# A written-out schedule with other prices for VectorE and GpSimd, and a regrouped softmax in sparse attention

## The chip, the cores and the metric

The kernel runs on one core of a Trainium2 chip. The metric is the device time of one execution in microseconds. One core has a matrix engine (TensorE, PE in the profile, with its weight loads as PEld), VectorE (DVE), ScalarE (ACT), GpSimd (POOL) and a queue for transfers (SyncE, SP). Each runs its own list of instructions in order, and an instruction waits for semaphores of the others.

## The reference

Two blocks of a transformer on 1024 positions of width 1024, in 32-bit floats. The first has two layers, each with two kinds of dense attention, a convolution and a gate; the second has a gated linear attention, an attention over keys that an indexer selects, and a feed-forward part. Cut to what the change touches, the sparse attention is this:

```python
def dsa_attention(q, ckv, iq, ik, iw):
    top_k = min(TOPK_MAX, L // 4)
    ...
    def one_block(args):
        s = jax.nn.relu(jnp.einsum('bqhd,bsd->bqhs', iq_b, ik).astype(jnp.float32))
        score = jnp.einsum('bqh,bqhs->bqs', iw_b.astype(jnp.float32), s)
        score = jnp.where(causal[None], score, -jnp.inf)
        _, idx = lax.top_k(score, top_k)
        kv_sel = jax.vmap(lambda c, i: c[i])(ckv, idx)
        logits = jnp.einsum('bqhc,bqkc->bqhk', q_b, kv_sel).astype(jnp.float32) * (dc ** -0.5)
        probs = jax.nn.softmax(logits, axis=-1).astype(kv_sel.dtype)
        return jnp.einsum('bqhk,bqkc->bqhc', probs, kv_sel)
```

It has 16 heads of a latent width of 128. The kernel computes it with masks in place of gathered keys.

## The kernel before

Activations lie transposed, features on the 128 partitions and positions along the columns, in pages (`pg`) of 128x512. Every operand of a matmul is split into a rounded part and a remainder (`split`, L720): a copy that rounds (a CAST in the profile, on VectorE or ScalarE) and a subtraction (`lo`), and a product is three matmuls. The subtraction runs on VectorE where the source is in PSUM, and on VectorE or GpSimd where it is in SBUF.

The program isn't written in the order in which it runs. Each helper records an operation with a price in microseconds for every engine that could run it (`alts`: t TensorE, a ScalarE, v VectorE, p GpSimd, d a transfer), what it reads and writes, and how to emit it. `schedule` (L406) then plays the whole program with these prices: each engine takes the earliest ready operation by its place in the text, within a window, if its buffers are free. An operation that two engines could run is left to the cheaper one if waiting for that would end earlier. The order that comes out is what is emitted; the chip then runs each engine's list in that order.

The prices are made in `c_act` (ScalarE, L266), `copy` (L302), `c_v` (VectorE, L314), `c_p` (GpSimd, L317), `scale` (L357), `red` (L370) and `vec` (L375). `LAT` (L485) is the time from an operation's end until another engine sees it. `o.dual` (L221) marks an operation that VectorE may run, that reads no PSUM and that has a source of over 64 columns; while GpSimd is busy, such an operation is priced longer:

```python
                    if e == "v" and o.dual and busy["p"] > now:
                        c += 0.42 * min(busy["p"] - now, c / 0.58)
```

The stages in order of time, roughly: first norm, modulation and convolution of block 1 (to 400 us), the two dense attentions of its first layer (`attend`, L1075; 350 to 900), the second layer (900 to 1800, its attentions 1200 to 1700), the indexer's scores and the search for the largest (1850 to 2300), run beside the gated linear attention, sparse attention (2300 to 2960), its projection and a norm (to 3140), the feed-forward part (to 3890) and a last gated addition with a norm (to the end). In the attentions a unit is a head and a chunk of 512 positions; a unit has a lead, a loop and an end, and the lead of the next unit is merged into the loop of this one (`pipeline`, L258).

In sparse attention (from L1757) a unit is a head and a half (c) of the 1024 positions. For each of four blocks of 128 queries (t) and one or two blocks of keys (b), the lead computes scores in PSUM, adds the mask and takes the maximum in one VectorE instruction (L1796, CUSTOM_DVE_ANT_0 with a read of the accumulator), makes -max/sqrt(128) (L352), the exponentials with their sums on ScalarE (L289), a reciprocal of the sum (L1807), and scales the probabilities by it (L365 on VectorE, L363 on ScalarE). Where there are two blocks of keys, two more operations of one column join the maxima and the sums (L330). The loop transposes the probabilities on TensorE (L393), splits them and multiplies by the values; the end adds two halves of the sum into `ob`, which is written out.

## Time and profile before

| | |
|---|---|
| median of 3 runs | 3984.7 us (3984.07 to 3984.71) |
| the profiled execution, its own time | 3984.33 us |
| its span, first to last instruction | 3982.5 us |
| busy: TensorE, VectorE, ScalarE, GpSimd | 97%, 79%, 49%, 38% of the span |
| mean granted TensorE clock | 0.99 of full speed |

Busy time is the union of an engine's instructions. A matmul's span in the profile holds its pipeline, so matmuls that follow each other overlap, and a TensorE that is busy all the time need not be at its peak. In the rows, L330 is an addition, subtraction or product of two tensors on VectorE and L332 the same on GpSimd; L340 multiplies by a column or tensor and adds or multiplies a second; L298 is a copy on VectorE; L373 a reduction; L389 a matmul and L393 a transpose. A tile's name is its kind: `pg` a page in SBUF, `ps` a PSUM bank, `sm` a small tile, `c` a constant.

### The profile page before, as it was taken

What the parts mean: (1) busy time and instruction counts of PE and PEld (TensorE: products, weight loads), DVE (VectorE), ACT (ScalarE), POOL (GpSimd) and SP (SyncE); (2) the same over time, 40 slices, a digit from 0 to 9 for tenths busy, and PEclk for the clock granted to TensorE, in tenths of its full rate; (3) what the DMA queues carried; (4) which work ended last, traced back from release to release, by engine and by line L of the source; (5) the groups of instructions that cost most, each with busy time, mean ns of one, the idle gap of its engine ahead of it and who ended that gap; (6) DMA issues with size and microseconds to landing.
All of it is one profiled execution on the core that took longest, in us unless ns stands there. A gap on an engine that the chain in (4) does not pass through costs nothing. (4 is left out here: it accounts for less than half of the span.)

```text
span 3982.5 us, 53245 instructions
## 1 busy us (share of the span) xinstructions
PE 3860.4 (97%) x18344; PEld 3100.5 (78%) x18344; DVE 3130.6 (79%) x5241; ACT 1964.9 (49%) x3841; POOL 1520.0 (38%) x1348
## 2 busy tenths in 40 slices
PE   6999999999999999999999999999999999999997
PEld 4778777768878777678988888877778788888876
DVE  8998899996796888857988985788776854446598
ACT  5345577763245566635355731566653432222255
POOL 7654465561252444522354531111143511111177
PEclk8999999999999999999999999999999999999998
DMA  7232222133232110232111332000054411111121
GB/s 247 82 119 79 63 68 65 47 115 135 69 121 72 31 30 20 87 116 73 57 55 60 126 111 77 29 29 34 25 191 127 146 42 49 51 51 43 49 86 57
DMA packets 184975, 311.82 MB, mean 78 GB/s; under 512 B 22912, under 2 KB 46208, under 8 KB 184704
## 3 DMA queue, kind: packets, MB, share of 16 engines
q1 hardware_dynamic: 184704, 308.42, 23.6%
q8 instruction: 144, 2.36, 0.2%
q14 instruction: 127, 1.04, 0.1%
HBM read 237.81 MB, written 62.39 MB: 75 GB/s over the span
## 5 line engine op out<-in xcount | busy, mean ns | idle before, releaser
L389 PE MATMUL ps<-pg,pg 128*128 128x512 f32 (+5 forms) x17008 | 3789.5, 384 | 43.6 <-ACT pg L289 19.8
L389 PEld LDWEIGHTS ps<-pg,pg 128*128 128x128 f32 (+3 forms) x17008 | 2955.4, 188 | 733.5 <-issue 72.9
L332 POOL TENSOR_TENSOR pg<-pg,pg 128x512 fp32r<-128x512 f32 (+4 forms) x1030 | 1437.2, 1411 | 2015.2 <-ACT pg L289 1037.8
L289 ACT ACTIVATE pg<-pg 128x512 fp32r<-128x512 f32 (+7 forms) x1385 | 785.7, 596 | 779.4 <-DVE pg L340 252.1
L289 ACT ACTIVATE pg<-ps 128x512 f32<-128x512 f32 (+10 forms) x1352 | 681.8, 551 | 870.3 <-PE ps L389 708.2
L330 DVE TENSOR_TENSOR pg<-pg,pg 128x512 fp32r<-128x512 f32 (+7 forms) x839 | 769.5, 930 | 150.9 <-ACT pg L289 99.2
L330 DVE TENSOR_TENSOR pg<-ps,pg 128x512 fp32r<-128x512 f32 (+9 forms) x650 | 367.5, 584 | 223.3 <-PE ps L389 133.9
L340 DVE SCALAR_TENSOR_TENSOR pg<-ux,c,pg 128x512 f32<-128x512 f32 x416 | 361.4, 895 | 22.5 <-ACT pg L289 13.9
L373 DVE TENSOR_REDUCE sm<-ps 128x1 f32<-128x512 f32 (+1 forms) x492 | 326.5, 681 | 26.8 <-PE ps L389 23.5
L298 DVE CAST pg<-pg 128x512 fp32r<-128x512 f32 (+4 forms) x342 | 210.9, 623 | 56.2 <-ACT pg L289 24.9
L340 DVE SCALAR_TENSOR_TENSOR pg<-pg,c,pg 128x512 f32<-128x512 f32 (+3 forms) x242 | 223.9, 962 | 5.6 <-ACT pg L289 4.9
L289 ACT ACTIVATE pg<-ps,c 128x512 f32<-128x512 f32 (+1 forms) x182 | 128.0, 708 | 202.9 <-PE ps L389 162.9
L393 PE MATMUL ps<-c,pg 128*128 128x128 f32 (+1 forms) x796 | 163.8, 272 | 11.4 <-DVE pg L298 6.0
L1541 DVE MAX8 sm<-ux 128x8 f32<-128x384 f32 (+5 forms) x192 | 166.9, 884 | 1.3
L1542 DVE MATCH_REPLACE8 ux<-sm,ux 128x384 f32<-128x384 f32 (+5 forms) x192 | 167.4, 875 | 0.0
L298 DVE COPY ux<-ps 128x512 f32<-128x512 f32 x79 | 54.5, 691 | 140.3 <-ACT pg L289 122.6
L389 PE MATMUL ps<-pg,c 128*128 128x512 f32 (+3 forms) x196 | 81.7, 482 | 54.8 <-DVE pg L330 21.7
L393 PEld LDWEIGHTS ps<-c,pg 128*128 128x128 f32 (+1 forms) x796 | 103.9, 141 | 37.9 <-DVE pg L298 6.0
L289 ACT ACTIVATE pg<-pg,sm 128x512 f32<-128x512 f32 (+2 forms) x192 | 116.3, 607 | 18.8 <-DVE sm L352 18.4
L678 ACT ACT_TABLE_LOAD x92 | 118.0, 1283 | 1.6
L383 POOL MEMSET pg<- 128x128 f32 (+2 forms) x193 | 49.9, 274 | 159.7 <-PE ps L389 99.0
L1796 DVE CUSTOM_DVE_ANT_0 pg<-ps,pg 128x512 f32<-128x512 f32 (+3 forms) x176 | 98.8, 573 | 11.6 <-PE ps L389 10.7
(73 smaller groups left out, 1024.7 us busy)
## 6 DMA issues: line engine op xcount, KB each, us to landing
d<-pg SPq DMA_DIRECT2D x202, 256.0 KB, 2.0
pg<-d SPq DMA_DIRECT2D x178, 256.0 KB, 3.5
pg<-in_w2a SPq DMA_DIRECT2D x108, 256.0 KB, 3.0
pg<-in_wmod SPq DMA_DIRECT2D x96, 256.0 KB, 3.3
pg<-in_wup SPq DMA_DIRECT2D x88, 256.0 KB, 2.7
pg<-in_win SPq DMA_DIRECT2D x80, 256.0 KB, 3.4
pg<-in_wout SPq DMA_DIRECT2D x64, 256.0 KB, 3.3
pg<-in_wdn SPq DMA_DIRECT2D x48, 256.0 KB, 2.7
```

The costliest lines, as they stand in the source:

```text
L289: nc.scalar.activation(real(out), real(in_), fn, scale=real(scale), **k)
L298: self.nc.vector.tensor_copy(real(out), real(in_))
L330: self.nc.vector.tensor_tensor(out=real(out), in0=real(in0), in1=real(in1), op=o)
L332: self.nc.gpsimd.tensor_tensor(out=real(out), in0=real(in0), in1=real(in1), op=o)
L340: self.nc.vector.scalar_tensor_tensor(out=real(out), in0=real(in0), scalar=real(scalar), in1=real(in1), op0=o0, op1=o1)
L373: lambda e: self.nc.vector.tensor_reduce(out=real(out), in_=real(in_), axis=AX.X, op=o))
L389: lambda e: self.nc.tensor.matmul(real(out), lhsT=real(lhsT), rhs=real(rhs), start=start, stop=stop))
L393: lambda e: self.nc.tensor.transpose(real(out), real(in_), real(ident)))
L678: nc.scalar.preload_act_table_set(pre)
L1541: P.vec(P.c_v(n), [w], [m8], lambda e, m8=m8, w=w: nc.vector.max(real(m8), real(w)))
L1542: P.vec(P.c_v(n), [w, m8], [w], lambda e, m8=m8, w=w: nc.vector.match_replace(real(w), real(m8), real(w), MARK))
L1796: lambda e, p=p, s=s, n=n, m=mk[t, b], a=sm[:, b:b + 1]: nc.vector.tensor_tensor_reduce(out=real(p), in0=real(s[:, 0:n]), in1=real(m), sca ...
```

## The change

Three things are edited. First, the prices: VectorE's, ScalarE's and GpSimd's fixed parts get smaller (an addition of 512 columns on VectorE goes from 0.687 to 0.599 us, on GpSimd from 1.326 to 1.218), and a new table `TAIL` adds a time after which the result counts as done, which doesn't hold the engine. Second, the rule for VectorE and GpSimd: `hold` is the time until which either holds the other off, and an operation of the one that is priced while the other holds is made longer by what is left. Reductions and what `vec` records (the largest-8 search, masked maxima, scans) don't take part. And GpSimd takes an operation that VectorE could run only if VectorE has enough ready work of the kind that takes no part. Third, sparse attention: one small tile holds the numbers of the four blocks; the maximum over two blocks of keys is carried by the second masked maximum, whose start value is the first's result; -max, the sum of two and the reciprocal are one operation for four blocks. The probabilities are no longer scaled. Instead the reciprocals are spread over 64 rows by four transposes into a PSUM bank, copied into a page `rr`, and multiplied into `ob` once for two heads.

```diff
     def c_act(self, n, src, extra=0):
-        return (n * 0.836 + (170 if isinstance(src, View) and src.psum else 202) + extra) / 1000
+        return (n * 0.836 + (49 if isinstance(src, View) and src.psum else 93) + extra) / 1000
...
     def c_v(self, n, ex=0):
-        return (n * 1.04 + 155 + ex) / 1000
+        return (n * 1.04 + 67 + ex) / 1000
 
     def c_p(self, n):
-        return (n * 2.2 + 200) / 1000
+        return (n * 2.2 + 92) / 1000
...
     def vec(self, cost, reads, writes, emit):
 
-        return self.op({"v": cost}, reads, writes, emit)
+        o = self.op({"v": cost}, reads, writes, emit)
+        o.dual = False
+        return o
...
+        TAIL = {"t": 0.0, "a": 0.115, "v": 0.083, "p": 0.08, "d": 0.0}
+        hold = {"v": 0.0, "p": 0.0}
...
                                 if wait + o.alts[m] < o.alts[e]:
                                     ok = False
+                                elif e == "p" and m == "v":
+
+                                    apart = sum(x.alts["v"] for _, x in ready["v"][:6] if not issued[x.idx] and not x.dual)
+                                    if hold["v"] <= now:
+                                        apart += max(0.0, busy["v"] - now)
+                                    if len(ready["v"]) > 1 and apart + o.alts["v"] < o.alts["p"] + max(0.0, hold["v"] - now):
+                                        ok = False
...
-                    if e == "v" and o.dual and busy["p"] > now:
-                        c += 0.42 * min(busy["p"] - now, c / 0.58)
+                    if e == "p" or e == "v" and o.dual:
+                        other = "p" if e == "v" else "v"
+                        c += max(0.0, hold[other] - now)
+                        hold[e] = now + c
...
-                        fin = now + c
+                        fin = now + c + TAIL[e]
...
+                sm = P.buf("sm", (128, 4, 4), F32)
+                nb = 1 + c
                 for t in range(4 * c, 4 * c + 4):
                     qs = slice((t % 4) * 128, (t % 4) * 128 + 128)
-                    sm = P.buf("sm", (128, 4, 4), F32).rearrange("p a b -> p (a b)")
-                    nb = 1 if t < 4 else 2
+                    top = sm[:, 0, t % 4:t % 4 + 1]
...
-                    if nb == 2:
-                        P.tt(sm[:, 0:1], sm[:, 0:1], sm[:, 1:2], "max")
-                    P.ts(sm[:, 2:3], sm[:, 0:1], -(128.0 ** -0.5), None, "mult")
+                P.ts(sm[:, 0, :], sm[:, 0, :], -(128.0 ** -0.5), None, "mult")
+                for t in range(4 * c, 4 * c + 4):
                     for b in range(nb):
-                        P.act(pn[t, b], pn[t, b], "Exp", bias=sm[:, 2:3], scale=128.0 ** -0.5, accum=sm[:, 4 + b:5 + b])
-                    if nb == 2:
-                        P.tt(sm[:, 4:5], sm[:, 4:5], sm[:, 5:6], "add")
-                    P.vec(0.08, [sm], [sm], lambda e, sm=sm: nc.vector.reciprocal(real(sm[:, 6:7]), real(sm[:, 4:5])))
-                    for b in range(nb):
-                        P.scale(pn[t, b], pn[t, b], sm[:, 6:7])
+                        P.act(pn[t, b], pn[t, b], "Exp", bias=sm[:, 0, t % 4:t % 4 + 1].k("e"), scale=128.0 ** -0.5,
+                              accum=sm[:, 1 + b, t % 4:t % 4 + 1].k((t, b)))
+                if nb == 2:
+                    P.tt(sm[:, 1, :], sm[:, 1, :], sm[:, 2, :], "add")
+                P.vec(0.2, [sm], [sm], lambda e, sm=sm: nc.vector.reciprocal(real(sm[:, 3, :]), real(sm[:, 1, :])))
...
+                rp = P.ps()
+                for t in range(4):
+                    P.tr(rp[0:64, t * 128:(t + 1) * 128], sm[:, 3, t:t + 1].to_broadcast([128, 64]), ident)
                 if i == 0:
-                    ob[c] = P.pg()
+                    ob[c], rr[c] = P.pg(), P.pg()
+                P.copy(rr[c][G, :].k(i), rp[0:64, :])
...
                 if i == 1:
+                    P.tt(ob[c], ob[c], rr[c], "mult", "vp")
                     obd[hp, c] = P.dram((128, 512))
```

What the planner makes of it shows in the order of the instructions on an engine. The end of GpSimd's list is the last norm, in which a page's mean is taken off and squares are summed; these are its last ten operations before:

```order
L332 TENSOR_TENSOR pg_38516<-pg_38516,pg_38649 128x256
L332 TENSOR_TENSOR pg_38675<-pg_38394,pg_38675 128x256
L332 TENSOR_TENSOR pg_38701<-pg_38409,pg_38701 128x256
L332 TENSOR_TENSOR pg_38516<-pg_38516,pg_38704 128x256
L332 TENSOR_TENSOR pg_38510<-pg_38510,pg_38698 128x256
L332 TENSOR_TENSOR pg_38510<-pg_38510,pg_38701 128x256
L332 TENSOR_TENSOR pg_38457<-pg_38457,pg_38724 128x256
L332 TENSOR_TENSOR pg_38549<-pg_38549,pg_38724 128x256
L332 TENSOR_TENSOR pg_38675<-pg_38675,pg_38724 128x256
L332 TENSOR_TENSOR pg_38701<-pg_38701,pg_38724 128x256
```

And these are its last ten in the change:

```order
L332 TENSOR_TENSOR pg_38142<-pg_38045,pg_38142 128x256
L332 TENSOR_TENSOR pg_37728<-pg_37728,pg_38174 128x256
L332 TENSOR_TENSOR pg_38217<-pg_38052,pg_38217 128x256
L332 TENSOR_TENSOR pg_38270<-pg_38063,pg_38270 128x256
L332 TENSOR_TENSOR pg_38166<-pg_38166,pg_38314 128x256
L332 TENSOR_TENSOR pg_38320<-pg_38079,pg_38320 128x256
L332 TENSOR_TENSOR pg_38162<-pg_38162,pg_38318 128x256
L332 TENSOR_TENSOR pg_38162<-pg_38162,pg_38320 128x256
L332 TENSOR_TENSOR pg_38122<-pg_38122,pg_38352 128x256
L332 TENSOR_TENSOR pg_38320<-pg_38320,pg_38352 128x256
```

Of the last eight subtractions of a mean (a tile with itself and one common tile: 38724 before, 38352 after) GpSimd had four and has two; the rest of its ten operations lie further back in the change than before.

In the attention of block 1's first layer, VectorE's list holds reductions of scores in PSUM (L373), splits of pages, and the modulation of the next layer (L340). Between two such reductions of the same unit it reads before (`sm` is the unit's tile of maxima):

```order
L298 CAST pg_7414<-pg_7401 128x512
L373 TENSOR_REDUCE sm_7390<-ps_7406 128x1
L298 CAST pg_7433<-pg_7408 128x512
L373 TENSOR_REDUCE sm_7390<-ps_7419 128x1
L330 TENSOR_TENSOR pg_7454<-pg_7079,pg_7138 64x512
L373 TENSOR_REDUCE sm_7390<-ps_7426 128x1
L330 TENSOR_TENSOR pg_7441<-pg_7441,pg_6388 64x512
L373 TENSOR_REDUCE sm_7390<-ps_7436 128x2
```

And in the change, for the same unit:

```order
L298 CAST pg_7478<-pg_7443 128x512
L373 TENSOR_REDUCE sm_7417<-ps_7437 128x1
L330 TENSOR_TENSOR pg_7497<-pg_7415,pg_7470 128x512
L373 TENSOR_REDUCE sm_7417<-ps_7445 128x2
L330 TENSOR_TENSOR pg_7514<-pg_7443,pg_7478 128x512
L373 TENSOR_REDUCE sm_7417<-ps_7455 128x1
L330 TENSOR_TENSOR pg_7528<-pg_7461,pg_7492 128x512
L373 TENSOR_REDUCE sm_7417<-ps_7474 128x1
```

The subtractions of the split (L330 of 128x512), which stood on GpSimd's list, now stand between the reductions on VectorE's.

In sparse attention, VectorE's list at the end of one unit's lead reads before (`sm` holds one block's numbers):

```order
L330 TENSOR_TENSOR sm_26012<-sm_26012 128x1
L330 TENSOR_TENSOR pg_26172<-ps_26102,pg_26164 64x512
L1807 RECIPROCAL sm_26012<-sm_26012 128x1
L330 TENSOR_TENSOR sm_26047<-sm_26047 128x1
L365 TENSOR_SCALAR pg_26011<-pg_26011,sm_26012 128x512
L1807 RECIPROCAL sm_26047<-sm_26047 128x1
L298 CAST pg_26191<-ps_26070 128x512
L365 TENSOR_SCALAR pg_26057<-pg_26057,sm_26047 128x384
```

And in the change (`sm` holds four blocks' numbers):

```order
L298 COPY pg_26431<-ps_26394 64x512
L330 TENSOR_TENSOR pg_26085<-ps_26394,pg_26431 64x512
L330 TENSOR_TENSOR pg_26085<-pg_26085,pg_26047 128x512
L298 CAST pg_26459<-ps_26415 128x512
L330 TENSOR_TENSOR sm_26284<-sm_26284 128x4
L330 TENSOR_TENSOR pg_26468<-ps_26411,pg_26457 128x512
L330 TENSOR_TENSOR pg_26474<-ps_26415,pg_26459 128x512
L1825 RECIPROCAL sm_26284<-sm_26284 128x4
L330 TENSOR_TENSOR pg_26484<-ps_26433,pg_26464 128x512
```

One addition and one reciprocal of four columns stand there instead of those of one column, the scalings (L365) are gone, and the third row is the product of `ob` with the reciprocals.

## Rows read from the trace of the kernel before

**Rows 1.** Stretches: length; busy us (count): PE, PEld, DVE, ACT, POOL; clock; DMA.

```profile
0.00:400.00 400.00, 357.79 (x1737) 284.40 (x1738) 366.18 (x484) 187.92 (x343) 233.21 (x173) 0.96 0.39 131
700.00:800.00 100.00, 99.53 (x442) 72.68 (x442) 95.89 (x160) 78.29 (x151) 52.64 (x47) 1.00 0.15 44
1300.00:1700.00 400.00, 395.24 (x1627) 283.43 (x1627) 339.38 (x538) 257.22 (x476) 185.22 (x180) 1.00 0.15 45
2500.00:2900.00 400.00, 390.83 (x2140) 318.85 (x2139) 320.50 (x1095) 255.83 (x664) 48.50 (x87) 1.00 0.09 30
3300.00:3400.00 100.00, 100.00 (x443) 82.81 (x442) 51.66 (x66) 30.60 (x48) 19.05 (x20) 1.00 0.16 51
3800.00:3900.00 100.00, 92.00 (x380) 72.36 (x379) 94.60 (x89) 50.57 (x80) 83.40 (x52) 0.95 0.17 53
3900.00:3982.50 82.50, 53.41 (x394) 49.81 (x392) 71.82 (x98) 44.90 (x86) 55.09 (x52) 0.81 0.18 61
```

**Rows 2.** The same for ten us with matmuls of 256 columns.

```profile
3940.00:3950.00 10.00, 10.00 (x86) 10.00 (x85) 8.74 (x12) 2.98 (x9) 9.36 (x12) 1.00 0.24 71
```

**Rows 3.** Groups of TensorE, 1300:1700: count | busy, mean ns | idle before.

```profile
L389 PE MATMUL ps<-pg,pg 128*128 128x512 f32 x878 | 308.5, 459 | 2.4 <-DVE pg L298 1.1 <-ACT pg L289 0.9 <-POOL pg L332 0.3
...
L389 PE MATMUL ps<-pg,pg 97*128 97x512 f32 x108 | 42.7, 421 | 0.1
```

**Rows 4.** Timeline of the tail: start, us, engine, operation, count.

```profile
3802.58 0.43 DVE L298 CAST pg<-pg 128x512 fp32r<-128x512 f32 x1 [0.81 <-POOL pg L332]
...
3888.52 0.74 DVE L340 SCALAR_TENSOR_TENSOR pg<-pg,c,pg 128x512 f32<-128x512 f32 x1
3888.67 8.53 POOL L332 TENSOR_TENSOR pg<-pg,pg 128x512 fp32r<-128x512 f32 x5 [0.36 <-DVE pg L298]
3889.18 6.87 DVE L340 SCALAR_TENSOR_TENSOR pg<-pg,pg 128x512 f32<-128x512 f32 x4
...
3897.68 0.68 DVE L340 SCALAR_TENSOR_TENSOR pg<-pg,pg 128x512 f32<-128x512 f32 x1
```

**Rows 5.** Timeline in the first layer's attention.

```profile
732.76 1.32 POOL L332 TENSOR_TENSOR pg<-pg,pg 128x512 fp32r<-128x512 f32 x1 [0.97 <-ACT pg L289]
...
732.96 1.89 DVE L373 TENSOR_REDUCE sm<-ps 128x2 f32<-128x512 f32 x3
```

**Rows 6.** Groups of VectorE and GpSimd, 500 to 900 us.

```profile
L340 DVE SCALAR_TENSOR_TENSOR pg<-pg,c,pg 128x512 f32<-128x512 f32 x72 | 69.9, 982 | 0.2
L298 DVE CAST pg<-pg 128x512 fp32r<-128x512 f32 x62 | 42.5, 690 | 5.3 <-ACT pg L289 4.6
...
L332 POOL TENSOR_TENSOR pg<-pg,pg 128x512 fp32r<-128x512 f32 x128 | 183.3, 1439 | 140.0 <-DVE pg L298 52.8 <-ACT pg L289 52.6 <-PE ps L389 14.9
```

**Rows 7.** Groups of small operations and scalings, 2500 to 2900 us, sparse attention.

```profile
L365 DVE TENSOR_SCALAR pg<-pg,sm 128x512 f32<-128x512 f32 x48 | 26.7, 555 | 0.5
...
L330 DVE TENSOR_TENSOR sm<-sm 128x1 f32<-128x1 f32 x113 | 20.1, 189 | 0.5 <-ACT pg L289 0.3
...
L1807 DVE RECIPROCAL sm<-sm 128x1 f32<-128x1 f32 x116 | 17.8, 156 | 1.8 <-ACT pg L289 1.1
...
L352 DVE TENSOR_SCALAR sm<-sm 128x1 f32<-128x1 f32 x117 | 16.1, 148 | 0.2
```

**Rows 8.** Timeline in sparse attention, transposes (L393) among matmuls.

```profile
2690.91 0.27 PE L393 MATMUL ps<-c,pg 128*128 128x128 f32 x1
...
2690.94 0.48 PE L389 MATMUL ps<-pg,pg 128*128 128x512 f32 x1
...
2691.26 0.27 PE L393 MATMUL ps<-c,pg 128*128 128x128 f32 x1
```

**Rows 9.** Groups of TensorE in the tail, 3800 us to the end.

```profile
L389 PE MATMUL ps<-pg,pg 128*128 128x512 f32 x368 | 88.7, 400 | 0.0
...
L389 PE MATMUL ps<-pg,c 128*128 128x512 f32 x12 | 10.5, 1026 | 18.7 <-DVE pg L330 15.6 <-POOL pg L332 3.1
L389 PE MATMUL ps<-pg,c 128*128 128x256 f32 x8 | 3.3, 526 | 8.3 <-POOL pg L332 8.3
```

More of the change, by code (lines that the diff above doesn't have):

```diff
@@ L352, in emit @@
             self.nc.vector.tensor_scalar(out=real(out), in0=real(in0), scalar1=real(s1), scalar2=real(s2), op0=o0, **k)
-        return self.op({"v": (out.n * (1.04 if in0.psum or accum is not None else 0.52) + 190 + (127 if accum is not None else 0)) / 1000},
+        return self.op({"v": (out.n * (1.04 if in0.psum or accum is not None else 0.52) + 110 + (90 if accum is not None else 0)) / 1000},
                        [in0, s1, s2], [out, accum], emit)
@@ L1757, in block2 @@
     for hp in range(8):
-        ob = {}
+        ob, rr = {}, {}
         cut = P.side()
@@ L1794, in block2 @@
                         p = P.pg()[:, 0:n]
-                        P.vec((n * 1.04 + 200) / 1000, [s, mk[t, b]], [p, sm[:, b:b + 1]],
-                              lambda e, p=p, s=s, n=n, m=mk[t, b], a=sm[:, b:b + 1]: nc.vector.tensor_tensor_reduce(
-                                  out=real(p), in0=real(s[:, 0:n]), in1=real(m), scale=1.0, scalar=BIG, op0=OP.add,
-                                  op1=OP.max, accum_out=real(a)))
+                        first = [top.k(t)] if b else []
+                        P.vec((n * 1.04 + 200) / 1000, [s, mk[t, b]] + first, [p, top.k(t)],
+                              lambda e, p=p, s=s, n=n, m=mk[t, b], a=top, b=b: nc.vector.tensor_tensor_reduce(
+                                  out=real(p), in0=real(s[:, 0:n]), in1=real(m), scale=1.0, scalar=real(a) if b else BIG,
+                                  op0=OP.add, op1=OP.max, accum_out=real(a)))
                         pn[t, b] = p
-                    if nb == 2:
-                        P.tt(sm[:, 0:1], sm[:, 0:1], sm[:, 1:2], "max")
-                    P.ts(sm[:, 2:3], sm[:, 0:1], -(128.0 ** -0.5), None, "mult")
+                P.ts(sm[:, 0, :], sm[:, 0, :], -(128.0 ** -0.5), None, "mult")
+                for t in range(4 * c, 4 * c + 4):
                     for b in range(nb):
-                        P.act(pn[t, b], pn[t, b], "Exp", bias=sm[:, 2:3], scale=128.0 ** -0.5, accum=sm[:, 4 + b:5 + b])
-                    if nb == 2:
-                        P.tt(sm[:, 4:5], sm[:, 4:5], sm[:, 5:6], "add")
-                    P.vec(0.08, [sm], [sm], lambda e, sm=sm: nc.vector.reciprocal(real(sm[:, 6:7]), real(sm[:, 4:5])))
-                    for b in range(nb):
-                        P.scale(pn[t, b], pn[t, b], sm[:, 6:7])
+                        P.act(pn[t, b], pn[t, b], "Exp", bias=sm[:, 0, t % 4:t % 4 + 1].k("e"), scale=128.0 ** -0.5,
[3 more added lines that the diff above has]
+                P.vec(0.2, [sm], [sm], lambda e, sm=sm: nc.vector.reciprocal(real(sm[:, 3, :]), real(sm[:, 1, :])))
                 lead = P.take(cut)
```

12 lines of the change are left out of this document (6 added, 6 removed).

## Prediction

> **What bounds the kernel now.** I first read the table of stretches [rows 1]. TensorE is marked busy in nearly all of most of them, but a matmul's time there includes its pipeline, so I count matmuls instead. In a stretch of the feed-forward part that has no other limit, 443 matmuls of 512 columns run in 100 us [rows 1], 0.226 us each; where the columns are 256, 86 run in 10 us [rows 2], 0.116 us each. Held against that, the attention of the second layer of block 1 (1300 to 1700 us) has 1627 matmuls, of which 878 + 296 + 120 + 108 = 1402 have 512 columns ([rows 1, 3]; of the four groups the first and the last stand there): 1402 x 0.226 + 225 x 0.12 = 344 us of work in 400 us. So about 56 us are lost there in waits too short to show as idle time. The tail (3800 to 3982.5 us) holds 12 + 368 + 384 + 8 matmuls ([rows 9], where three of the four groups stand), 380 x 0.226 + 392 x 0.116 = 131 us of work in 182.5 us: 51 us lost. The feed-forward stretch loses nothing. TensorE is the bound in general, and what can be gained is what it loses where VectorE, ScalarE and GpSimd are late.
>
> There VectorE is the busiest: 95.89 of 100 us in the attention of the first layer, 339 of 400 in that of the second, 94.60 of 100 and 71.82 of 82.5 in the tail, 366 of the first 400 [rows 1]. Much of that is waiting for GpSimd. In the tail five GpSimd operations take 8.53 us while four VectorE operations take 6.87 us [rows 4]: they go in turn, 1.71 us for one of each, and the same operation takes VectorE 0.68 us when it runs by itself [rows 4]. An operation that reads PSUM is not held up: three reductions take 1.89 us although a GpSimd operation of 1.32 us starts 0.2 us before them [rows 5]. These three also start (1.89 - 0.68) / 2 = 0.60 us apart, shorter than the 0.67 to 0.69 us of one: the planner's old price (0.69) is the duration, its new one (0.60) the pitch.
>
> **The change part by part.** *The work that moves.* By the two orders, GpSimd's tensor operations fall from 1083 to 507. Where VectorE and GpSimd go in turn, a moved operation replaces a pair of 1.71 us by two VectorE operations of 0.60 to 0.68 us each: 1.20 to 1.36, a gain of 0.35 to 0.5, say 0.45 us. Where GpSimd hid behind VectorE's reads of PSUM, a moved operation costs VectorE 0.60 us more. The bound from both sides is therefore -0.5 to +0.6 us of VectorE time for each of the 576, and it is decided stretch by stretch.
>
> *Tail.* Counted operation by operation in the two orders, 90 leave GpSimd after 3800 us and 13 come to it; 77 net, some 42 of 512 columns and 35 of 256. The turns are nearly permanent there, so VectorE gains 42 x 0.45 + 35 x 0.22 = 27 us of its 166. The two longest idle groups of TensorE there are 18.7 us (15.6 behind VectorE's additions) and 8.3 us (behind GpSimd's) [rows 9], both ended by these operations. I take 20 us of the 27 as on the path, bounds 0 (the chain of normalisations sets the pace whatever the engine) and 35. **-20 us.**
>
> *The first 400 us.* 133 leave GpSimd and 11 come back; VectorE is at 366 of 400, most of it the convolution, which TensorE doesn't wait for until its layer ends. 122 x 0.45 = 55 us of VectorE time, of which I take a fifth to be on the path. **-12 us**, bounds 0 and -25.
>
> *The two attentions of block 1.* In 500 to 900 us, 105 leave GpSimd and 15 come; 68 copies go from VectorE to ScalarE and 38 the other way. VectorE gets 90 x 0.60 = 54 us more, loses 30 copies x 0.5 = 15, and loses part of its waiting: 72 x (0.982 - 0.74) and 62 x (0.690 - 0.43), both against the time of the same operation by itself [rows 4, 6], are 17 + 16, with the additions (some 19 by the same reckoning) 52 us, of which the moved 90 of the 168 GpSimd operations (their largest group, 128, is in [rows 6]) carry 28. 54 - 15 - 28 = +11 us in 400: VectorE goes from 374 to some 385, which is **no relief**. What is left is that a moved operation ends in 0.68 instead of 1.44 us, that the other GpSimd operations are placed under reductions, and that the planner's times are now the pitches. Per attention 50 to 80 us are lost; I take a tenth of the roughly 130 us together, **-15 us**, bounds -55 (half) and +25 (VectorE at 100% in the first layer's attention and the rest of the waits unchanged).
>
> *Sparse attention, VectorE and ScalarE.* Per head and half, scaling of the probabilities (L365, L363), four -max, four reciprocals and the two-block additions go; one of each for four blocks comes instead. In 2500 to 2900 us that is 16.1 + 17.8 + 20.1 + 26.7 us and 16 us of the narrower scalings off VectorE [rows 7], 97 us of 320.5 busy; coming back are 28 copies of 64x512 shared with ScalarE (0.6 to 0.69), 14 products (0.69 or, on GpSimd, 1.3) and some 70 operations of 4 columns at about 0.15: 30 us. VectorE gets 65 us lighter in 400 [rows 1].
>
> *Sparse attention, TensorE.* 128 transposes are added (4 in each of 32 units), which put the reciprocals along the rows of the result. In the trace a transpose starts at 2690.91, the next matmul 0.03 us later, and the next transpose 0.32 us after that, where a matmul of 512 columns alone would take 0.226 [rows 8]: 0.03 + 0.09 = 0.12 us for one transpose between matmuls. 128 x 0.12 = **+15 us**, all of it on the engine that sets the pace. The Trainium skill (TensorE: Matmul & The Clock Gate, Part 4: PE-mode transpose) gives about 275 ns for a 128x128 transpose in a kernel's context; by that the added work would be 128 x 0.275 = 35 us, an estimate from that page, and the sum below 20 us worse; the profile lists 0.27 us as one such instruction's duration too, but the starts in the trace give the 0.12.
>
> Against it stands what this stretch loses: with 0.12 for each transpose the 2140 matmuls of the 400 us come to some 380 us, so 20 in 400 and about 25 over the whole part are lost. With VectorE at 64% instead of 80% I take half of that, **-12 us**, bounds 0 and -22. The new copy takes one of the eight PSUM banks for a while in each unit, and the exponentials wait for the largest of four blocks; both are covered by the next unit's scores, which are merged into this unit's loop, and cost up to 8 us if that cover is thin.
>
> *The rest* (projections, gated linear attention, output parts): the same moves where TensorE loses some 50 us in all; **-8 us**, bounds -20 and +5. In the feed-forward part the moves hide behind a full TensorE: 0. DMA traffic is the same 1400 transfers.
>
> Sum: -20 - 12 - 15 + 15 - 12 - 8 = **-52 us**. The profiled execution took 3984.33 us (its span and 1.8 us around it), the median of the runs is 3984.7, so the forecast is 3984.7 - 52 = 3932.7, rounded to **3930 us**.
>
> **The rivals.** *A, the attentions gain for real:* the plan is right at last, and half of the 130 us lost there goes, -60 instead of -15, with the tail at -35: 3930 - 45 - 15 = 3870, with the good ends of the others 3860. For it: GpSimd's operations of 1.44 us stand between ScalarE and TensorE in that loop. Against it: VectorE's load doesn't fall.
>
> *B, only the ends gain:* the attentions give 0, sparse attention pays its transposes and wins nothing (+15), the tail and the start give half: 3984.7 - 10 - 6 + 15 - 8 = 3975. Against it: VectorE's 65 us.
>
> *C, slower:* VectorE becomes the bound in the attention of the first layer. It is at 95.89 of 100 us now, and work worth 54 us moves onto it in 400. If the GpSimd operations that stay still collide as now, the 28 us of relief are not there: 374 + 54 - 15 = 413 of 400, +13 us, about +20 with the 100 us before and the like in the second layer; with 15 for the transposes, and the ends unchanged, 3984.7 + 35 = 4020. It decides from the point where VectorE has over 97% in those stretches. Against it: the planner's new rule sends an operation to GpSimd only where VectorE has enough that isn't in its way.
>
> *D, nothing comes of it:* the order changes all over, but TensorE is full in most of the span and what the edges gain the transposes take: 3984.
>
> **How the numbers follow.** Forecast 0.48, A 0.14, B 0.14, D 0.07, C 0.17. A difference of 0.2%, 8 us, is about what a measurement of this kernel can tell from no change. Faster: 0.48 + 0.14 + 0.14 = 0.76; within it 0.07; slower 0.17. The range takes in A's 3860 and, with D and B, the near part of C up to 3995; what lies beyond on both sides is some 2 in 10.
>
> **What would show it.** Right: in the tail, VectorE's operations of 512 columns near 0.7 us instead of 1.1 to 1.4, and its stretch about 20 us shorter; VectorE in the attentions still above 90%, with TensorE's matmul count per 100 us up by 1 to 2%; in sparse attention VectorE under 70%, the transposes interleaved at 0.12 us, and the part's length unchanged within 10 us. Wrong: attentions shorter by over 40 us (A) or longer (C), sparse attention longer by over 20 us (the transposes dearer, or PSUM banks waited for), or VectorE operations still at 1.3 us beside the GpSimd operations that stay.

## The result, and the profile after

The changed kernel runs in 3927.81 us (median of four runs, 3927.69 to 3928.23) against 3984.7 us before: a ratio of 0.9855, with a 95% interval from 0.9843 to 0.9866. The forecast was 3930 us. The profiled execution has a span of 3925.9 us; these are the head of its page and the stretches that answer to [rows 1].

```profile
span 3925.9 us, 52648 instructions
...
PE 3854.2 (98%) x18472; PEld 3105.0 (79%) x18472; DVE 3023.2 (77%) x5354; ACT 1961.4 (50%) x3852; POOL 723.7 (18%) x772
```

```profile
0.00:400.00 400.00, 377.09 (x1863) 304.26 (x1864) 343.94 (x627) 206.51 (x372) 56.05 (x57) 0.97 0.41 137
700.00:800.00 100.00, 98.81 (x437) 71.17 (x436) 95.78 (x171) 78.23 (x155) 20.11 (x24) 1.00 0.18 55
1300.00:1700.00 400.00, 395.36 (x1632) 285.45 (x1631) 331.45 (x551) 262.40 (x486) 91.03 (x105) 1.00 0.18 54
2500.00:2900.00 400.00, 400.00 (x2270) 328.10 (x2269) 284.31 (x768) 229.73 (x602) 61.66 (x101) 1.00 0.13 46
...
3800.00:3900.00 100.00, 99.24 (x591) 87.50 (x590) 94.99 (x169) 60.84 (x102) 25.42 (x13) 1.00 0.17 54
3900.00:3925.90 25.90, 7.59 (x50) 6.49 (x49) 19.85 (x47) 15.93 (x35) 7.58 (x8) 0.68 0.24 81
```

In the first 400 us TensorE issues 1863 matmuls where it issued 1737, although VectorE is busy 22 us less and runs 143 operations more. The 591 against 380 in the 100 us from 3800 are not the same work: 344 of the 591 have 256 columns, and 7 of the 380. In the attentions the counts hardly move (437 against 442, 1632 against 1627), so the 1 to 2% more that the prediction named as a sign did not come.

A stretch at a fixed time holds other work once the kernel is shifted, so I cut both kernels at marks that bound nearly the same work of TensorE (1775 matmuls up to the first mark before, 1771 after): the first and last reduction (L373) of each attention, the first masked maximum of sparse attention and its last, and the first load of the weights for the last gate. The table has the length of each part before in us, and what each kernel adds or takes.

| | start | attention 1 | between | attention 2 | indexer, gated linear | sparse | projection, feed-forward | tail | span |
|---|---|---|---|---|---|---|---|---|---|
| before | 408.3 | 461.7 | 395.5 | 417.6 | 818.3 | 428.4 | 861.3 | 191.4 | 3982.5 |
| after | -26.3 | +4.4 | -9.3 | +3.8 | +7.3 | -6.0 | -5.2 | -25.3 | -56.6 |
| e1_sched | -28.2 | +4.4 | -9.5 | +2.7 | +8.8 | -16.9 | -4.0 | -25.3 | -68.0 |
| e2_dsa | +0.1 | -0.4 | +2.8 | -0.1 | 0.0 | -5.6 | +3.0 | +0.4 | +0.2 |
| e3_tail | -1.2 | -0.2 | -0.2 | -0.2 | 0.0 | +1.3 | +0.1 | -12.2 | -12.6 |
| e4_head | -8.7 | +17.7 | -0.3 | 0.0 | +0.5 | +1.5 | 0.0 | -0.1 | +10.6 |
| e5_prices | +20.0 | +28.0 | +7.2 | +11.0 | +25.0 | -10.1 | +3.8 | +0.1 | +85.0 |
| e6_rule | -10.1 | +18.5 | -16.8 | -2.9 | +5.3 | -1.1 | +2.1 | -13.5 | -18.5 |
| e7_nopool | -5.7 | +25.7 | -18.4 | -3.7 | +89.3 | +6.0 | +10.1 | -12.2 | +91.1 |
| e10_gla | -26.1 | +4.5 | -8.4 | +2.8 | +0.6 | -17.0 | -4.1 | -25.3 | -73.0 |
| e11_nolimit | +4.3 | +7.8 | -11.5 | +1.6 | +3.1 | -13.1 | -2.3 | +2.4 | -7.7 |
| e12_limit | -28.1 | +11.5 | -13.2 | +15.8 | +31.4 | -13.0 | -4.2 | -19.4 | -19.2 |

So 52 of the 57 us come from the two ends. The two attentions, for which 15 us were forecast, became 8 us longer together.

### The profile page after: what moved, and what is told of

Read it like the earlier page. It is cut to its first block, busy times and chain, and to the rows that moved or that the text cites. A ratio compares the mean times of both kernels' runs of the same rounds, so it can differ in the third digit from the quotient of the medians.

```text
span 3925.9 us, 52648 instructions
## 1 busy us (share of the span) xinstructions
PE 3854.2 (98%) x18472; PEld 3105.0 (79%) x18472; DVE 3023.2 (77%) x5354; ACT 1961.4 (50%) x3852; POOL 723.7 (18%) x772
## 4 chain that ended last, share of the span: by engine, by line
PE 74%; DVE 10%; ACT 3%; issue 1%; DMA 1%; POOL 0%; SPq 0%; ACTq 0%; DVEq 0%; POOLq 0%
PE ps L391 71%; DVE pg L330 4%; PE ps L395 3%; ACT pg L289 2%; DVE pg L340 2%; DVE sm L373 2%; DVE pg L298 0%; DVE sm L1555 0%; DVE ux L1556 0%; ACT L692 0%; DVE pg L1631 0%; DMA ux<-d 0%; DVE pg L352 0%; DMA pg<-in_wout 0%; DMA pg<-in_win 0%
## 5 line engine op out<-in xcount | busy, mean ns | idle before, releaser
L391 PE MATMUL ps<-pg,pg 128*128 128x512 f32 (+4 forms) x17008 | 3807.3, 385 | 42.0 <-ACT pg L289 19.1
L332 POOL TENSOR_TENSOR pg<-pg,pg 128x512 fp32r<-128x512 f32 (+4 forms) x467 | 648.7, 1395 | 2517.6 <-ACT pg L289 1383.7
L330 DVE TENSOR_TENSOR pg<-pg,pg 128x512 fp32r<-128x512 f32 (+9 forms) x1418 | 974.1, 711 | 162.8 <-ACT pg L289 110.1
L330 DVE TENSOR_TENSOR pg<-ps,pg 128x512 fp32r<-128x512 f32 (+9 forms) x650 | 369.8, 584 | 211.3 <-PE ps L391 144.5
L373 DVE TENSOR_REDUCE sm<-ps 128x1 f32<-128x512 f32 (+1 forms) x492 | 325.6, 680 | 21.7 <-PE ps L391 19.3
L340 DVE SCALAR_TENSOR_TENSOR pg<-ux,c,pg 128x512 f32<-128x512 f32 x416 | 320.7, 793 | 18.1 <-ACT pg L289 11.4
L298 DVE CAST pg<-pg 128x512 fp32r<-128x512 f32 (+5 forms) x261 | 125.5, 486 | 88.5 <-ACT pg L289 45.4
L340 DVE SCALAR_TENSOR_TENSOR pg<-pg,c,pg 128x512 f32<-128x512 f32 (+3 forms) x242 | 167.8, 728 | 6.5 <-ACT pg L289 6.1
L1555 DVE MAX8 sm<-ux 128x8 f32<-128x896 f32 (+5 forms) x192 | 167.4, 883 | 2.1 <-DMA ux<-d 0.3
L1556 DVE MATCH_REPLACE8 ux<-sm,ux 128x896 f32<-128x896 f32 (+5 forms) x192 | 167.3, 873 | 0.0
L289 ACT ACTIVATE pg<-pg,sm 128x512 f32<-128x512 f32 (+1 forms) x192 | 115.6, 605 | 29.3 <-DVE sm L352 29.0
L298 DVE CAST pg<-ps 128x512 fp32r<-128x512 f32 (+4 forms) x84 | 45.8, 552 | 72.9 <-PE ps L395 38.5
L340 DVE SCALAR_TENSOR_TENSOR pg<-ps,c,pg 128x512 f32<-128x512 f32 (+1 forms) x66 | 46.2, 706 | 58.6 <-PE ps L391 57.0
```

The lines of the kernel that those rows point to most:

```text
L289: nc.scalar.activation(real(out), real(in_), fn, scale=real(scale), **k)
L298: self.nc.vector.tensor_copy(real(out), real(in_))
L330: self.nc.vector.tensor_tensor(out=real(out), in0=real(in0), in1=real(in1), op=o)
L332: self.nc.gpsimd.tensor_tensor(out=real(out), in0=real(in0), in1=real(in1), op=o)
L340: self.nc.vector.scalar_tensor_tensor(out=real(out), in0=real(in0), scalar=real(scalar), in1=real(in1), op0=o0, op1=o1)
L373: lambda e: self.nc.vector.tensor_reduce(out=real(out), in_=real(in_), axis=AX.X, op=o))
```

## The experiments

The theory after the result: the schedule does it, by keeping VectorE and GpSimd out of each other's way where VectorE is nearly always busy, and the regrouped softmax pays for its transposes. The rivals: the lighter softmax carries part of the gain; the better prices alone do it; or all that matters is that less work stands on GpSimd.

### The two halves of the change

**e1_sched** has the prices and both rules, with the old softmax. **e2_dsa** has the old schedule with the regrouped softmax alone.

> The new prices, the new rule for VectorE and GpSimd and the table TAIL, with the sparse attention of before. Theory 1 (the gain comes from the schedule at the two ends of the program, 26 us up to the attentions and 25 us after the last weights are asked for; sparse attention in its new form gives 6 us): 3984.7 - 51 = about 3934. Rival (the regrouped softmax carries a good part, since VectorE gets lighter there): 3950 or more.

> Only the regrouped softmax in sparse attention, with the schedule's prices and rules of before. Theory 1: sparse attention gains about 6 us and nothing else moves: 3979. Rival A (the transposes at 0.12 us each are all that is felt): 3984.7 + 15 - 12 = 3988 as in the prediction. Rival B (the schedule's share is smaller than it looks): 3965.

The schedule alone gives 3917.23 us, a ratio of 0.9828 (0.9813 to 0.9842): 10.6 us faster than the whole change, and faster than the 3934 us expected. The softmax alone gives 3981.65 us, 0.9992 (0.9983 to 1.0002), which is no difference. It does shorten sparse attention under the old schedule, from 428.4 to 422.8 us, as its lighter VectorE should. But the new schedule brings that part to 411.5 us with the old softmax, and to 422.4 us with the new one. The stretch from 2500 to 2900 us in e1_sched:

```profile
2500.00:2900.00 400.00, 397.52 (x2195) 327.12 (x2194) 331.39 (x1132) 277.21 (x703) 56.65 (x100) 1.00 0.16 54
```

VectorE is at 83% here, more than the 80% before, and TensorE gets 2195 matmuls through, 55 more than before [rows 1]. TensorE's waits between the first and the last masked maximum are 0.7 us in all, and 9.4 before. So under the new schedule VectorE's load does not hold TensorE up. The 2270 matmuls of the changed kernel contain 116 of the new transposes, and TensorE is marked busy in all of the 400 us. The regrouped softmax alone, between its own first and last masked maximum (e2_dsa), shows the same:

```profile
2503.80:2926.60 422.80, 422.80 (x2395) 349.01 (x2394) 300.01 (x812) 236.84 (x628) 77.45 (x112) 1.00 0.14 47
```

TensorE is marked busy throughout, and the part takes 422.8 us here and 422.4 in the changed kernel. With this softmax the schedule makes no difference to the part, and with the old one it is worth 16.9 us.

### Which part of the softmax costs the ten microseconds

**e8_twice** is the changed kernel with each new transpose done twice into the same place. **e9_share** is the changed kernel with the small operations shared by four blocks, but the probabilities scaled as before the change, without the transposes, their copy and the product.

```diff
-                    P.tr(rp[0:64, t * 128:(t + 1) * 128], sm[:, 3, t:t + 1].to_broadcast([128, 64]), ident)
+                    for _ in range(2):
+                        P.tr(rp[0:64, t * 128:(t + 1) * 128], sm[:, 3, t:t + 1].to_broadcast([128, 64]), ident)
```

```diff
+                for t in range(4 * c, 4 * c + 4):
+                    for b in range(nb):
+                        P.scale(pn[t, b], pn[t, b], sm[:, 3, t % 4:t % 4 + 1])
...
-                rp = P.ps()
-                for t in range(4):
-                    P.tr(rp[0:64, t * 128:(t + 1) * 128], sm[:, 3, t:t + 1].to_broadcast([128, 64]), ident)
...
-                P.copy(rr[c][G, :].k(i), rp[0:64, :])
...
-                    P.tt(ob[c], ob[c], rr[c], "mult", "vp")
```

> The changed kernel with each of the 128 new transposes done twice into the same place, so 128 more on TensorE and nothing else. If one costs 0.085 us where TensorE is full (the masked maxima's span is 422.4 us with the new form and 411.5 us with the old one, both under the new schedule): 3927.8 + 11 = 3939. As priced in the prediction, 0.12: 3943. As the skill's page has it, 0.275: 3963. If what the new form costs is the PSUM bank or the copy and not the transposes: 3928 to 3932.

> The changed kernel with the new schedule, in which the small operations of sparse attention stay shared by four blocks, but the probabilities are scaled by the reciprocals as before the change, and the 128 transposes, the copy of their result and the product with it are left out. The changed kernel runs in 3927.8 us, the schedule alone with the old softmax in 3917.2. If the ten us between them are the transposes on a full TensorE, this runs in 3912 to 3918 us, masked maxima spanning 407 to 413 us. If they come from the exponentials waiting for the largest of four blocks, it stays at 3925 to 3930 us, with 420 us or more for that part, although VectorE has the scalings to do again.

With double transposes it takes 3942.91 us (0.9895, 0.988 to 0.9909), and sparse attention 437.3 us instead of 422.4: 14.9 / 128 = 0.116 us for each added transpose, the 0.12 read from starts [rows 8]. Among its matmuls stands the row of one, with a matmul 0.03 us behind it and the next transpose 0.34 after its own start:

```profile
2601.30 0.27 PE L395 MATMUL ps<-c,sm 128*64 128x128 f32 x1
2601.33 0.47 PE L391 MATMUL ps<-pg,pg 128*128 128x512 f32 x1
2601.64 0.27 PE L395 MATMUL ps<-c,sm 128*64 128x128 f32 x1
```

Without transposes, e9_share takes 3917.85 us (0.9831, 0.9816 to 0.9845) and sparse attention 411.9 us, the same as e1_sched within 0.6 us. So sharing the small operations brings nothing and costs nothing, and the exponentials that wait for four blocks are covered. The ten microseconds are the transposes and what belongs to them, 10.5 / 128 = 0.08 us each for the first set, less than for the second. TensorE's 2.5 idle us in 400 of e1_sched can cover only part of that difference, 4.4 us in all.

### Prices, exclusion, limit

Four kernels take the schedule apart, all with the old softmax. **e5_prices** has only the new prices and `TAIL`. **e6_rule** has both rules with the old prices and no `TAIL`. **e11_nolimit** has the new prices and the exclusion (`hold`), without GpSimd's limit. **e12_limit** has the new prices and the limit, but makes operations longer by the old rule. Against e1_sched, the last two edits are these:

```diff
-                                elif e == "p" and m == "v":
+                                elif False:
```

```diff
+                    if e == "v" and o.dual and busy["p"] > now:
+                        c += 0.42 * min(busy["p"] - now, c / 0.58)
                     if e == "p" or e == "v" and o.dual:
-                        other = "p" if e == "v" else "v"
-                        c += max(0.0, hold[other] - now)
                         hold[e] = now + c
```

> Only the numbers: the new fixed prices and TAIL; the old rule for VectorE beside GpSimd (0.42 of the overlap), no limit on what GpSimd takes, sparse attention as before. Theory 2 (what counts is that the plan's order fits the engines' pace; the load that leaves GpSimd is a consequence): most of the 68 us of the schedule, 3935 to 3945. Theory 1 (GpSimd's load in the tail and the start is the cause): GpSimd keeps most of its operations, so 3975 or more.

> Only the rules: VectorE and GpSimd exclude each other in the plan and GpSimd takes less, at the old prices without TAIL; sparse attention as before. Theory 1 (load and exclusion are the cause): 3920 to 3940. Theory 2 (pace of the prices): 3965 to 3985, since an operation of VectorE is still planned at 0.69 instead of 0.60 us.

> The schedule alone (old softmax) without GpSimd's limit: new prices and the rule that the two engines exclude each other, with GpSimd at about as many operations as before the change (1077). If the gain comes from a plan that knows of the exclusion, most of the 67 us stay: 3920 to 3940 us. If it comes from taking work off GpSimd, the time goes back towards the kernel before, 3970 to 3990 us.

> The schedule alone (old softmax) with the new prices and GpSimd's limit, but priced by the old rule: a VectorE operation is made longer beside a busy GpSimd, a GpSimd operation never beside VectorE. New prices alone gave 4069 us, with the full exclusion 3978, with exclusion and limit 3917. If the limit is what makes the new prices pay (few operations are left that could collide), this runs in 3915 to 3930 us. If the plan also has to know of the exclusion, it is 3945 to 3990 us.

(Where the exclusion is left out, the old rule for VectorE stays.)

| old softmax | neither rule | exclusion only | limit only | both |
|---|---|---|---|---|
| new prices | 4069.17 (1.021, 1.0195 to 1.0226) | 3978.03 (0.9981, 0.9972 to 0.999) | 3965.61 (0.9952, 0.9936 to 0.9969) | 3917.23 (0.9828) |
| old prices | 3984.7, the kernel before, with its own rule | | | 3964.56 (0.9947, 0.9931 to 0.9964) |

The new prices, though nearer to the 0.60 us at which VectorE's operations follow each other in the trace, cost 84 us by themselves. GpSimd keeps 970 tensor operations. The old rule makes an addition of 0.60 us on VectorE at most 0.42 x 0.60 / 0.58 = 0.43 us longer in the plan, and an operation of GpSimd never. In the trace of e5_prices, from 500 to 900 us, GpSimd's subtractions take 1.47 us where 1.22 is planned, and VectorE's 1.05:

```profile
L340 DVE SCALAR_TENSOR_TENSOR pg<-pg,c,pg 128x512 f32<-128x512 f32 x77 | 66.7, 874 | 0.3
L330 DVE TENSOR_TENSOR pg<-pg,pg 128x512 fp32r<-128x512 f32 x35 | 36.9, 1053 | 1.3 <-ACT pg L289 0.6
```

```profile
L332 POOL TENSOR_TENSOR pg<-pg,pg 128x512 fp32r<-128x512 f32 x104 | 152.1, 1470 | 170.7 <-ACT pg L289 71.7 <-DVE pg L298 47.7 <-issue 21.3
```

That this gap makes the loss is argued, not shown. What the runs show is that the exclusion takes 91 us back at the same prices, although GpSimd then has more operations (1077 in e11_nolimit).

Either rule takes that loss back, and only both together give the full gain; the table of parts shows that each serves other parts.

The prices are a cause of their own on top of the rules: e6_rule, which has both rules, differs from e1_sched in the prices and `TAIL` alone and is 47 us slower, just below the range expected if the pace of the prices counts. Up to the first reduction of attention 1, first e6_rule and then e1_sched:

```profile
0.00:398.20 398.20, 361.94 (x1775) 292.35 (x1776) 330.64 (x602) 193.43 (x363) 40.48 (x54) 0.95 0.40 135
```

```profile
0.00:380.10 380.10, 357.63 (x1771) 288.26 (x1772) 333.39 (x610) 198.27 (x358) 52.97 (x54) 0.97 0.42 141
```

GpSimd has 54 instructions in both and VectorE nearly the same time, yet the start is 18 us shorter with the new prices: what they change here is the order more than the load. In the first 400 us TensorE waits 12.5 us for VectorE's additions and 22.7 for ScalarE in e6_rule, 4.4 and 14.4 in e1_sched. Sparse attention follows the prices too: -1.1 us by the rules alone, -10.1 by the prices alone, -16.9 by both.

Without the limit (e11_nolimit) the start and the tail gain nothing, +4.3 and +2.4 us, against -28.2 and -25.3 with it: GpSimd keeps 1077 operations, and in the first 400 us VectorE is as busy as in the changed kernel, with fewer operations:

```profile
0.00:400.00 400.00, 358.59 (x1709) 282.95 (x1710) 343.29 (x429) 195.20 (x364) 255.66 (x180) 0.95 0.38 128
```

343 us for 429 operations, and 344 us for 627 after the change. TensorE's waits in those 400 us, as engine and line waited for, total, times and longest, start in e11_nolimit with these:

```profile
PE ps L391 <- ACT pg L289: 23.0, 10, 8.7
PE ps L391 <- POOL pg L332: 13.3, 7, 4.6
```

Without the exclusion (e12_limit) the start has its 28 us but the middle loses: attention 1 is 7 us, attention 2 is 13 us and the indexer's part 23 us longer than in e1_sched, although GpSimd has about as many operations there. In the indexer's part TensorE waits 11.1 us for ScalarE, in e1_sched 3.2. As I read it, the plan has a GpSimd operation and what follows it end too early; no run separates that further. So neither rule is the cause alone, and nor are the prices: e11_nolimit ran as if it were all the work taken off GpSimd, e12_limit as if it were the exclusion.

### Is it only that less stands on GpSimd?

Three kernels are the kernel before with GpSimd kept from operations that VectorE could run: **e3_tail** from the last gate on, **e4_head** in the first norm, modulation and convolution, **e7_nopool** everywhere.

```diff
                         ok = admissible(o, e)
+                        if e == "p" and "v" in o.alts and o.idx >= 27900:
+                            ok = False
```

(in e4_head the last condition is `o.tag in ("emb", "nm0", "mod0", "cin0", "in0", "conv0")`, in e7_nopool there is none.)

> The kernel before, with one line in the planner: from the last group of the feed-forward part on (operations 27900 to 29252 of the text) GpSimd takes nothing that VectorE could run. Prices as before. Theory 1 (in the tail VectorE and GpSimd go in turn, and a moved operation gives back 0.45 us): the tail is 20 to 27 us shorter, 3984.7 - 25 = 3960, and nothing before 3790 us changes. Rival (the right prices make the better order, taking GpSimd out by itself overloads VectorE): 3980 or slower.

> The kernel before, with GpSimd kept from all that VectorE could run in the parts up to the attentions (first norm, modulation, convolution, projections of layer 0). Theory 1 (the same turns at the start): 26 us less up to the first reduction of the attention, which the rest keeps, 3984.7 - 26 = 3959. Rival (as in the prediction: a fifth of the 55 us of VectorE time lies on the path): 3973. Rival 2 (prices and order made the start shorter, not the load of GpSimd): 3984.

> The kernel before, with GpSimd kept from everything that VectorE could run, in the whole program; old prices and rules. Theory 1 (less on GpSimd is what counts): 3940 or less, tail 12 us shorter as when only the tail was kept off GpSimd. Theory 2 and the prediction's rival C (VectorE becomes the bound in the attentions): the attentions get longer, the whole 4000 or more.

e3_tail gives 3973.32 us (0.9976, 0.9966 to 0.9985): 12.2 us less in the tail, half of what the change gives there. VectorE's additions of 512 columns take 0.69 us, about as long as one by itself [rows 4], but alone it is late for the last norm. TensorE's matmul groups from 3800 us in e3_tail, where [rows 9] has idle times of 18.7 and 8.3:

```profile
L389 PE MATMUL ps<-pg,c 128*128 128x512 f32 x12 | 5.6, 592 | 0.0
L389 PE MATMUL ps<-pg,c 128*128 128x256 f32 x8 | 4.1, 671 | 21.9 <-DVE pg L330 21.9
```

e4_head is slower, 3999.3 us (1.0032, 1.0021 to 1.0043): the start is 8.7 us shorter, but attention 1 gets 17.7 us longer, and none of the three times expected came. Why attention 1 gets longer no run shows. In the first 400 us TensorE no longer waits for GpSimd but 23 us for VectorE:

```profile
PE ps L389 <- DVE pg L330: 14.5, 6, 6.1
PE ps L389 <- ACT pg L289: 14.1, 6, 6.6
PE ps L389 <- DVE pg L298: 8.2, 1, 8.2
```

e7_nopool is at 4075.9 us (1.0228, 1.0213 to 1.0243), 89 us of it in the part of the indexer, where VectorE also searches the largest 8. Its worst stretch there:

```profile
2300.00:2400.00 100.00, 70.28 (x295) 55.61 (x294) 94.36 (x149) 31.14 (x65) 0.00 (x0) 0.83 0.22 78
```

So taking work off GpSimd is not the cause by itself. It pays in part, some 12 us in the tail and 6 to 9 at the start, and it costs 89 us in the indexer's part, where VectorE has long work that is not in GpSimd's way.

### The indexer's part

The changed kernel takes 7.3 us longer than the one before from the end of attention 2 to sparse attention. The longest wait of TensorE there in the changed kernel, and the hundred microseconds around it:

```profile
1867.93 58.27 PE L391 MATMUL ps<-pg,pg 128*128 128x512 f32 x337 [5.13 <-DVE pg L330]
```

```profile
1850.00:1950.00 100.00, 94.87 (x517) 82.13 (x516) 98.58 (x222) 37.88 (x79) 30.90 (x25) 0.98 0.17 53
```

VectorE is at 98.58% and TensorE waits 5.13 us for one of its additions or subtractions (L330). **e10_gla** is e1_sched without GpSimd's limit for the gated linear attention and the indexer:

```diff
-                                elif e == "p" and m == "v":
+                                elif e == "p" and m == "v" and o.tag not in ("gla", "glap", "idx"):
```

> The schedule alone (old softmax), in which GpSimd's limit does not hold for the gated linear attention and the indexer, so that GpSimd may take an operation there without VectorE having work of the other kind ready. From the first reduction of the last attention to sparse attention the schedule alone takes 827 us where the kernel before takes 818. If the limit puts too much on VectorE there, as leaving GpSimd out altogether did (908 us), this gives the 9 us back: 3906 to 3911 us. If the 9 us come from the prices or the order, it stays at 3915 to 3919 us.

It runs in 3908.97 us (0.9807, 0.9791 to 0.9824), and the part takes 818.9 us against 827.1 in e1_sched. The same hundred microseconds in e10_gla:

```profile
1850.00:1950.00 100.00, 99.27 (x568) 87.07 (x567) 96.88 (x204) 35.66 (x79) 38.35 (x30) 1.00 0.17 58
```

568 matmuls instead of 517, with five more operations on GpSimd. This version, the new schedule with the old softmax and the limit lifted there, is faster than the kernel before and the changed one.

## Why the prediction came out right, point by point

The forecast of 3930 us was 2 us off. That is luck in part. The sum of the terms was -52 us and the change measured is -57; the start, the tail and sparse attention gave 29 us more than forecast, and the two attentions 23 us less.

**Tail: -20 forecast, -25.3 measured, right in mechanism.** VectorE's operations of 512 columns, which took 1.12 to 1.39 us from 3800 us on before, are near 0.75 after, and GpSimd has 28 operations in this part instead of 105. Two of the groups before, then three after:

```profile
L330 DVE TENSOR_TENSOR pg<-pg,pg 128x512 f32<-128x512 f32 x31 | 42.2, 1387 | 4.3 <-ACT pg L289 3.9
L340 DVE SCALAR_TENSOR_TENSOR pg<-pg,c,pg 128x512 f32<-128x512 f32 x24 | 25.8, 1124 | 0.0
```

```profile
L330 DVE TENSOR_TENSOR pg<-pg,pg 128x512 f32<-128x512 f32 x46 | 33.4, 772 | 1.2 <-ACT pg L289 1.2
...
L340 DVE SCALAR_TENSOR_TENSOR pg<-pg,c,pg 128x512 f32<-128x512 f32 x24 | 17.3, 754 | 0.1
L330 DVE TENSOR_TENSOR pg<-pg,pg 128x512 fp32r<-128x512 f32 x20 | 13.9, 726 | 0.3 <-ACT pg L289 0.3
```

Of the two waits that I took 20 us from [rows 9], the first is gone and the second is left; from 3760 us on in the changed kernel:

```profile
L391 PE MATMUL ps<-pg,c 128*128 128x512 f32 x12 | 5.7, 601 | 0.8 <-DVE pg L330 0.8
L391 PE MATMUL ps<-pg,c 128*128 128x256 f32 x8 | 3.3, 526 | 8.6 <-POOL pg L332 8.6
```

VectorE is busy 22 us less in the tail (173.17 and 151.26 us), where 27 were forecast. At the old prices nearly as much relief gives only half of the gain: 153.77 us and -12.2 in e3_tail, 153.71 and -13.5 in e6_rule. The forecast priced the relief and not what the new prices add.

**First 400 us: -12 forecast, -26.3 measured, mis-sized, and with one cause left out.** The term took 55 us of VectorE's time as saved and a fifth of it as on the path, with the argument that TensorE does not wait for the convolution until its layer ends. The bound of -25 just missed the result. Up to the first reduction VectorE was saved 37 us, before and then after:

```profile
0.00:408.30 408.30, 365.40 (x1775) 290.50 (x1776) 370.57 (x490) 191.69 (x351) 236.17 (x176) 0.96 0.39 131
```

```profile
0.00:382.00 382.00, 359.09 (x1771) 289.08 (x1772) 333.65 (x609) 197.78 (x358) 53.30 (x54) 0.97 0.42 140
```

The same relief at the old prices, some 40 us of VectorE's time (329.61 us in e4_head and 330.64 in e6_rule instead of 370.57), makes the start 8.7 and 10.1 us shorter, about what the term gave. The rest comes only with the new prices (e1_sched), and the forecast had no term for what they do to the order here. The waits of TensorE in the first 400 us, before and then after, show that it did wait for VectorE and GpSimd, against the argument:

```profile
PE ps L389 <- ACT pg L289: 17.5, 5, 10.2
PE ps L389 <- POOL pg L332: 7.7, 4, 4.2
PE ps L393 <- DVE pg L298: 6.0, 1, 6.0
PE ps L389 <- DVE pg L298: 5.4, 6, 1.7
PE ps L389 <- DVE pg L330: 4.7, 5, 2.2
```

```profile
PE ps L391 <- ACT pg L289: 14.7, 6, 8.8
PE ps L391 <- DVE pg L330: 4.5, 7, 1.6
PE ps L395 <- DVE pg L298: 2.4, 2, 1.6
PE ps L391 <- DVE pg L298: 1.3, 1, 1.3
```

GpSimd's 7.7 us are gone, and VectorE's 16.1 are 8.2. I had read only VectorE's busy share, not who waited for it.

**The two attentions: -15 forecast, +8.2 measured, the step that failed.** The load was read rightly as "no relief": +11 us of VectorE's time was worked out for 400 us, and it is +4 over attention 1. Between the marks VectorE has, in before and after, in attention 1:

```profile
408.30:870.00 461.70, 455.47 (x2034) 337.47 (x2033) 431.65 (x682) 324.96 (x632) 254.58 (x238) 1.00 0.22 67
```

```profile
382.00:848.10 466.10, 456.17 (x2027) 335.06 (x2027) 435.39 (x746) 337.23 (x663) 128.24 (x143) 1.00 0.22 66
```

93% of the part in both, with nearly the same matmuls, and half the busy time on GpSimd. The operations did get shorter, as the groups from 500 to 900 us show beside [rows 6]:

```profile
L330 DVE TENSOR_TENSOR pg<-pg,pg 128x512 fp32r<-128x512 f32 x110 | 80.2, 738 | 4.2 <-PE ps L391 1.8 <-ACT pg L289 0.9 <-issue 0.4
L340 DVE SCALAR_TENSOR_TENSOR pg<-pg,c,pg 128x512 f32<-128x512 f32 x70 | 51.9, 755 | 0.2
...
L298 DVE CAST pg<-pg 128x512 fp32r<-128x512 f32 x37 | 17.6, 480 | 2.8 <-ACT pg L289 2.1 <-PE ps L391 0.3
```

But I added a gain for shorter times from ScalarE to TensorE on top, a tenth of what is lost there, for which no row spoke. It did not come. In e7_nopool, with none of these operations on GpSimd, attention 2 is 3.7 us shorter and attention 1 is 25.7 us longer, though VectorE is busy 91% of it. So neither GpSimd's load nor VectorE's share explains the length. Which dependence sets the pace of the attentions is still open: no run here made both shorter by as much as a microsecond.

**Sparse attention: +15 and -12 forecast, +3 together, -6.0 measured.** The price of a transpose held (e8_twice). The other term came for another reason than the one given: the stalls go by the schedule alone, 16.9 us in e1_sched with VectorE at 83%, and e2_dsa, which makes VectorE lighter, gains 5.6 net of its transposes. The two gains would add up to 22 us and together give 6.0, so both remedies treat one loss. VectorE is at 71% where 64% was forecast, and under 70% was the sign. By the 0.275 us of the Trainium skill (TensorE: Matmul & The Clock Gate, Part 4: PE-mode transpose) the sum would have been 20 us worse, an estimate from that page; e8_twice measures 0.116.

**The rest: -8 forecast, -7.2 measured (-9.3, +7.3 and -5.2).** The sum agrees, while the parts do not: I had not seen that the limit on GpSimd would leave TensorE waiting for VectorE in the indexer's part.

The rivals: A (attentions gain) and D did not come. Of B, only the statement on the attentions came, with more at the ends than it allowed. C's mechanism, VectorE as the bound because of what moves onto it, did appear, at 98.58% and past its own point of 97%, but in the indexer's part and at 7 us. In e7_nopool it is 89 us.

## What to carry to other kernels

Prices in a planner that are nearer to the pace of one engine by itself can make a schedule worse: here by 2% while the plan kept its old rule for two engines that hold each other off. On top of the new rules the same prices were worth 47 us. Change prices and rules together, and time each without the other. The same relief of an engine can be worth twice as much in another order, so ask who waits for it and not only how busy it is. In this kernel it paid to take work off the engine that holds the other off where the other is full of operations of the same kind, and to leave it there where the other has long work that is not disturbed. Two changes that treat the same loss don't add up: time each half by itself before both are kept.

## What the runs showed of the hardware

I had taken it that VectorE and GpSimd go in turn [rows 4]. In the changed kernel's tail they do not always. Here two GpSimd operations came while VectorE had a dense list, and were done only behind it:

```profile
3848.16 9.60 POOL L332 TENSOR_TENSOR pg<-pg,pg 128x512 f32<-128x512 f32 x2 [20.13 <-ACT pg L289]
3848.66 0.68 DVE L340 SCALAR_TENSOR_TENSOR pg<-pg,pg 128x512 f32<-128x512 f32 x1
3849.26 1.88 DVE L330 TENSOR_TENSOR pg<-pg,pg 128x512 f32<-128x512 f32 x3
...
3854.68 0.68 DVE L340 SCALAR_TENSOR_TENSOR pg<-pg,pg 128x512 f32<-128x512 f32 x1
3856.54 1.76 DVE L340 SCALAR_TENSOR_TENSOR pg<-pg,pg 128x512 f32<-128x512 f32 x1 [1.19 <-POOL pg L332]
```

From 3848.66 to 3854.68, eleven VectorE operations start 0.60 us apart, none longer than by itself, while two GpSimd operations take 9.60 us together; then VectorE itself has to wait for the result. The Trainium skill (SBUF — State Buffer, SBUF: two separate sides) says that the shared pair of ports is an exclusive lock which the first to start holds for its whole instruction, while the other blocks. The trace agrees that one blocks; it adds that the one that waits need not be next. Why it was turn by turn in [rows 4] and not here is open.

The clock went with the waits: the granted clock of the tail's 191.4 us was 0.89 before, 0.91 in the 179.2 us of e3_tail, and it is 0.95 in the 166.1 us after, so in part of the tail matmuls run at 2.4 instead of 1.2 GHz. In e7_nopool's stretch above, where TensorE is busy 70.28 of 100 us, it is 0.83.
